# S5 tables of an encoder trunk: products moved from GpSimd to VectorE, sums to accumulating DMAs

## Chip, cores and metric

The kernel runs on 1 core of one Trainium2 chip. The metric is the device time of one execution in microseconds (us). The time before is the median of 3 runs, 1194.32 us (1193.07 to 1194.72). "Contended" below means that VectorE and GpSimd work at the same moment.

## The reference, cut to what matters

One layer, 1024 tokens of width 1024, in float32:

```python
n = rmsnorm(h, norm1_g); proj = n @ w_in
xa, ga, ub, pc = split(proj)          # RG-LRU input and gate, S5 input, Hyena inputs
ya = rglru_mixer(xa, ga, ...)         # conv, 4 gate products, forward and backward linear recurrence
yb = s5_mixer(ub, ...)                # below
yc = hyena_mixer(pc, ...)             # conv, long filter by FFT
h = h + concat(rms(ya), rms(yb), rms(yc)) * g @ w_out
h = h + conv_ffn(rmsnorm(h), ...);    return rmsnorm(h)
```

The S5 mixer has 24 groups of 16 channels, each with one diagonal complex state of 64 values, run forward and backward. The kernel cuts the 1024 tokens into 128 chunks of 8. What a state gets from a chunk, and what a chunk gets from a state, are then small matrices: a power (0 to 8) of the state's complex decay times an entry of B or C. These matrices are the tables of this case.

## The kernel before

**Stages.** `program` (L1459) first normalises x and transposes it. It then walks over 15 column blocks of `w_in` (`names`, L1489: ub0, xa0, ub1, ub2, ga0, xa1, x10, v0, ga1, ...), each in two halves of 512 tokens. One half is 24 matmuls (`columns`, L692: every float32 product is made of three matmuls on a high and a low part, `mm3`, L96). Behind each block its consumer takes the PSUM result: `s5_in` for ub, `rg_conv` for xa, `rg_gate` for ga, `hy_in` for the Hyena blocks. All S5 and RG-LRU work lies between these blocks. Later come the Hyena transforms, the output projection (`wo`) and the ConvFFN, which takes the second half of the time.

**What sets the order.** TensorE's order is the program's own (L1463). The dictionary `before` (L1565) writes it by hand: the entry 2i + half names what is issued ahead of that half of block i. On every other engine the compiler's scheduler picks the order of the queue by its own simulated times, so work that is ready sooner can be issued ahead of work that stands earlier in the program. `tc.issue_after(ins)` puts what a block of code issues on the engine of `ins` behind `ins` in that engine's queue; it is an order in the queue, and no wait for a result. `after` (L1466) opens it for several instructions.

**S5's parts**, for six batches b of 4 groups:

- `prep` (L153), once, on VectorE, makes the powers LPr and LPi and copies them (L279 to L283) into `s5pw` and `s5ow` as (power j, group g), so that the 8 powers of one group lie 24 elements apart.
- `comb` (L302) makes one table of 128 x 512 (4 groups x 16 channels x 8 powers): a product `out = w1 m1` and a product `ox = w2 m2` (L308), and their sum or difference (L310), all on the engine that it is given.
- `lag_prep` (`lp`, L321) makes two tables, Or and Oi, by `comb` on GpSimd, and stores both to DRAM (`s5ot`, L326, on SyncE's DMA queue).
- `lags` (`lg`, L328) multiplies Or and Oi with B on TensorE (`lk`, L339).
- `tables` (`tb`, L364) makes two tables `wn` by `comb`, on VectorE for b below 2 and on GpSimd for the others. It makes the angles `ang` (L380 to L382, VectorE), their sines on ScalarE, and R (L389, a GpSimd product that only spreads rho over 128 columns).
- `transposed` (`wt`) transposes wn on TensorE; `states` (`st`, L432) makes the chunk states: matmuls S, rotations `pr` on VectorE (L451 to L454), scans G (L467, L469), rotations `hr` (L451 to L454); `outputs` (`ou`, L476) multiplies into Y (L485 to L487).

The tables live in a pool of 23 half-size buffers (`half`, L64, L1523), used in turn; a new tile waits until the old one in its buffer has been read.

**The RG-LRU's first input.** `rg_conv` (L740) for block xa0 makes the convolution u (ScalarE L706, VectorE L712 three times), splits it into uh (ScalarE, L87) and ul (VectorE, L88 in `split`), and splits the gate weights wg in the same way. `scan(0, 0)`, at entry 6, multiplies uh and ul with wg (tile `gate`): TensorE issues it right behind the 48 matmuls of block ub1.

**Weights.** Most weight blocks are split by `dsplit` (L90): ScalarE writes lo = -raw, a DMA on GpSimd's queue adds raw onto lo (L93, `accum_op=ALU.add`), and ScalarE writes hi. This accumulating DMA is the kind that the change uses for sums.

Of the kernel before, what the change touches and what calls it, by code (L numbers as in the profile page):

```python
# [10 lines left out]
F32 = mybir.dt.float32  # L11
F32R = mybir.dt.float32r
AF = mybir.ActivationFunctionType
ALU = mybir.AluOpType
# [3 lines left out]
P = 128  # L18
# [9 lines left out]
NG = 24  # L28
# [5 lines left out]
class K:  # L34
# [50 lines left out]
    def split(self, hi, lo, raw, eng=None):  # L85

        self.nc.scalar.activation(hi, raw, AF.Identity)  # L87
        (eng or self.nc.vector).tensor_tensor(lo, raw, hi.bitcast(F32), op=ALU.subtract)  # L88

    def dsplit(self, hi, lo, raw):  # L90

# [14 lines left out]
def bc(ap, *shape):  # L106
    return ap.to_broadcast(list(shape))
# [36 lines left out]
class S5:  # L144
# [8 lines left out]
    def prep(self, tp):  # L153

        k = self.k
        nc = k.nc
        pp = self.pool
        p = self.p1
# [4 lines left out]
        V = nc.vector  # L163
        cnt = [0]

        def t(shape=(P, NG), name=None):
            cnt[0] += 1
            return (pp if name else tp).tile(list(shape), F32, name=name or f"s5t{cnt[0]}")
# [6 lines left out]
        def mul(a, b, out=None):  # L175
            return tt(a, b, ALU.mult, out)
# [91 lines left out]
        for m in (1, 2, 4):  # L268
            S = (P, m, NG)
            cmul(LPr[:, 1:1 + m], LPi[:, 1:1 + m], bc(LPr[:, m:m + 1], *S), bc(LPi[:, m:m + 1], *S),  # L270
                 LPr[:, 1 + m:1 + 2 * m], LPi[:, 1 + m:1 + 2 * m], S)
        m2 = mul(mag, mag)
# [2 lines left out]
        mul(m4, m4, self.rho)  # L275
        self.PW, self.OW = [], []
        for i, LP in enumerate((LPr, LPi)):
            w = t((P, 8, NG), f"s5pw{i}")
            V.tensor_copy(w[:64], LP[:64, 7::-1])  # L279
            V.tensor_copy(w[64:], LP[64:, 0:8])  # L280
            o = t((P, 8, NG), f"s5ow{i}")
            V.tensor_copy(o[:64], LP[:64, 1:9])
            V.tensor_copy(o[64:], LP[64:, 8:0:-1])  # L283
            self.PW.append(w)
            self.OW.append(o)

        self.B2 = []
# [11 lines left out]
        self.Cn = t(S3, "s5cn")  # L299
        V.tensor_scalar(self.Cn, self.ci, -1.0, None, op0=ALU.mult)  # L300

    def comb(self, eng, out, b, w1, m1, w2, m2, op):  # L302

        sh = (P, GB, 16, 8)
        g = slice(GB * b, GB * b + GB)
        x = self.k.half("ox", shape=sh)
        for o, w, m in ((out, w1, m1), (x, w2, m2)):
            eng.tensor_tensor(o, bc(w[:, :, g].rearrange("p j g -> p g j").unsqueeze(2), *sh),  # L308
                              bc(m[:, g].unsqueeze(3), *sh), op=ALU.mult)
        eng.tensor_tensor(out, out, x, op=op)  # L310

    def out_matrix(self, b):

        OT = []
        for n, m1, m2 in (("Or", self.cr, self.ci), ("Oi", self.Cn, self.cr)):
            o = self.k.half(n, shape=(P, GB, 16, 8))
            self.comb(self.k.nc.gpsimd, o, b, self.OW[0], m1, self.OW[1], m2, ALU.subtract)
            OT.append(o)
        return OT

# [43 lines left out]
    def tables(self, b):  # L364

        k = self.k
        nc = k.nc
        S = (P, GB, P)
        V, G = nc.vector, nc.gpsimd
        g = slice(GB * b, GB * b + GB)  # L370
        t = self.tab[b] = {}

        t["W"] = []
        for m1, m2, op in ((self.Gr, self.Gi, ALU.subtract), (self.Gi, self.Gr, ALU.add)):
            w = k.half("wn", shape=(P, GB, 16, 8))
            self.comb(V if b < 2 else G, w, b, self.PW[0], m1, self.PW[1], m2, op)
            t["W"].append(w)

        ang, rnd = k.half("ang", shape=S), k.half("rnd", shape=S)
        V.tensor_tensor(ang, bc(self.f8s[:, g].unsqueeze(2), *S), bc(self.nt.unsqueeze(1), *S), op=ALU.mult)  # L380
        V.tensor_scalar(rnd, ang, MAGIC, -MAGIC, op0=ALU.add, op1=ALU.add)
        V.tensor_tensor(ang, ang, rnd, op=ALU.subtract)  # L382
        Es, Ec, R = t["Es"], t["Ec"], t["R"] = [k.half(n, shape=S) for n in ("Es", "Ec", "R")]
        one = k.col(1.0, "c_one")
        nc.scalar.activation(Es, ang, AF.Sin, scale=2.0 * PI_LO)
        nc.scalar.activation(Ec, ang, AF.Sin, scale=PI_LO)
        nc.scalar.activation(Ec, Ec, AF.Square)
        nc.scalar.activation(Ec, Ec, AF.Identity, scale=-2.0, bias=one)
        G.tensor_tensor(R, bc(self.rho[:, g].unsqueeze(2), *S), bc(one, P, 512).rearrange("p (g n) -> p g n", n=P),  # L389
                        op=ALU.mult)  # L390
        G.memset(R[0:64, :, 0], 0.0)
        G.memset(R[64:128, :, 127], 0.0)

# [213 lines left out]
class Net:  # L607
# [132 lines left out]
    def rg_conv(self, ct, ps):  # L740
        k = self.k
        u = self.conv(ps, [self.c("rcw", 3 * j + ct) for j in range(4)], self.c("rcb", ct), 1, "u")
        uh, ul = k.slot("uh", F32R), k.slot("ul", F32R)
        k.split(uh, ul, u)
        wgs = []
        for d in range(2):
            wg = k.half("wg", F32R, (P, 2, 256))
            raw = k.half("wgr", shape=(P, 256))
            k.nc.sync.dma_start(raw, self.I["gates"][ct][:, 256 * d:256 * d + 256])
            k.split(wg[:, 0], wg[:, 1], raw)  # L750
            wgs.append(wg)
        return u, uh, ul, wgs
# [359 lines left out]
class Ffn:  # L1112
# [36 lines left out]
    def second(self, ns):  # L1149
# [11 lines left out]
        for kt in range(4):  # L1161
            p12, p22 = self.transposes(ns, kt), self.transposes(ns, kt + 4)
            g1, g2 = self.net.c("n2", kt), self.net.c("n2", kt + 4)
            b22 = k.half("b22")
            nc.scalar.activation(b22, p22, AF.Identity, scale=g2)  # L1165
            t1, t3 = k.half("t1"), k.half("t3")
            V.scalar_tensor_tensor(t1, p12, g1, f(self.B11[kt][0]), op0=ALU.mult, op1=ALU.subtract)
            V.scalar_tensor_tensor(t3, p12, g1, b22, op0=ALU.mult, op1=ALU.subtract)
            split(self.B22[kt], b22, V)
            V.tensor_tensor(t1, t1, f(self.B11[kt][1]), op=ALU.subtract)  # L1170
            t2 = k.half("t2")
            V.tensor_tensor(t2, b22, t1, op=ALU.subtract)
            split(self.T2[kt], t2, V)
            split(self.T3[kt], t3, V)
            split(self.T1[kt], t1, G)
            G.tensor_tensor(t2, f(self.B21[kt][0]), t2, op=ALU.subtract)
            G.tensor_tensor(t2, t2, f(self.B21[kt][1]), op=ALU.add)
            split(self.T4[kt], t2, V)
            yield
# [279 lines left out]
def program(ctx, tc, I, O, dbg=None):  # L1459
    k = K(ctx, tc)  # L1460
    nc = k.nc
    net = Net(k, I, O)
    ctx.enter_context(tc.manual_schedule(engines={mybir.EngineType.PE}))  # L1463

    @contextmanager
    def after(*instructions):  # L1466

        with ExitStack() as st:
            for i in instructions:
                st.enter_context(tc.issue_after(i))  # L1470
            yield
# [16 lines left out]
    x = [k.slot(f"x{i}") for i in range(8)]  # L1488
# [66 lines left out]
    def load(src, o):  # L1555
        for i in range(src.shape[0]):
# [3 lines left out]

    lp, lg, il, tb, wt, st, lo = (s5.lag_prep, s5.lags, s5.intra_load, s5.tables, s5.transposed, s5.states,
                                  s5.load_out)
    lu, ou = lambda b: s5.load_u(b, part(ud, b)), lambda b: s5.outputs(b, part(yd, b))

    before = {  # L1565
        2: [(lp, 0), (lp, 1)],
        4: [(lp, 2), (net.hy_layer, 1)],
        6: [(scan, 0, 0)],
        7: [(lg, 0), (tb, 0)],
        8: [(tb, 1), (lg, 1)],  # L1570
        9: [(il, 0), (scan, 0, 1), (lp, 3)],
        10: [(lg, 2)],
        11: [(wt, 0), (lu, 0), (lo, 0)],
# [187 lines left out]
```

## Time and profile before

| what | us |
|---|---|
| median of 3 runs | 1194.32 |
| the profiled execution, its own time | 1192.28 |
| its span, first to last instruction | 1190.5 |
| granted TensorE clock, mean over the span | 0.958 of full speed |

One execution was profiled; all times within it are in us from the first instruction. The trace gives each instruction with its engine, its line, the tiles that it writes and reads (out<-in), its duration and what ended the idle time before it. PE is TensorE, PEld its weight loads, DVE VectorE, ACT ScalarE, POOL GpSimd, SPq and POOLq the DMA queues of SyncE and GpSimd. A line such as L88 or L308 is that of a helper, so the tile tells what it serves. Merged rows (x2, x24) give a common start and total length.

### The profile page before, as it was taken

How to read it: one execution, taken by the hardware profiler on the slowest of the kernel's cores; microseconds unless marked ns; L12 is line 12 of the kernel's file. 1: busy time of each engine (PE TensorE's matmuls, PEld its weight loads, DVE VectorE, ACT ScalarE, POOL GpSimd, SP SyncE). 2: the span in 40 equal slices, each digit the busy share in tenths (PEclk: the TensorE clock that was granted, in tenths of full speed). 3: DMA queues.
4: the chain of work that ended last, by engine and by line, in shares of the span. 5: the costliest groups of instructions: out<-in, count | busy, mean ns of one | idle time of the engine just before them, and what ended most of it. 6: DMA issues, size and time to landing. Idle time of an engine off the chain costs nothing.

```text
span 1190.5 us, 13485 instructions
## 1 busy us (share of the span) xinstructions
PE 1083.7 (91%) x4938; PEld 880.1 (74%) x4938; DVE 1016.7 (85%) x1246; ACT 543.1 (46%) x757; POOL 441.2 (37%) x330
## 2 busy tenths in 40 slices
PE   5849989987998989968999999999999998999896
PEld 4638877766686778756878888888888876888785
DVE  6997689998879984997989898988989899578975
ACT  6429566555241550643434343343434353545453
POOL 6285375342317442375433232323232234011002
PEclk8969999988988999988999999999999999999998
DMA  6233724525736151311322222222212590455003
GB/s 246 62 107 90 219 56 134 131 77 159 257 110 237 36 198 52 158 36 35 106 80 80 89 72 92 79 95 71 89 71 89 190 357 18 135 142 114 1 1 142
DMA packets 58511, 134.27 MB, mean 113 GB/s; under 512 B 10923, under 2 KB 19499, under 8 KB 58444
## 3 DMA queue, kind: packets, MB, share of 16 engines
q1 hardware_dynamic: 53116, 114.00, 27.9%
q0 software_dynamic: 5328, 19.40, 7.0%
q8 instruction: 39, 0.64, 0.2%
q14 instruction: 28, 0.23, 0.1%
HBM read 96.24 MB, written 30.33 MB: 106 GB/s over the span
## 4 chain that ended last, share of the span: by engine, by line
PE 45%; DVE 21%; issue 11%; ACT 3%; POOL 2%; DMA 2%; SPq 0%; POOLq 0%; DVEq 0%; ACTq 0%
PE p L97 31%; PE dn L97 5%; PE wo L97 5%; DVE dr L1299 2%; DVE dw L88 2%; PE x L97 1%; DVE G L469 1%; DMA wor<-in_w_out 1%; DVE T L1159 1%; DVE S L88 1%; DVE hrm L451 1%; DVE hrn L453 1%; DVE cv L712 1%; DVE B L1159 1%; DMA dr<-gd 1%
## 5 line engine op out<-in xcount | busy, mean ns | idle before, releaser
L97 PE MATMUL dn<-dw 128*128 128x512 f32 x924 | 213.8, 393 | 10.0 <-DVE dw L88 9.9
L97 PEld LDWEIGHTS dn<-dw 128*128 128x128 f32 x924 | 173.9, 189 | 49.7 <-DVE dw L88 13.3
L97 PE MATMUL p<-T,S 128*128 128x512 f32 x792 | 188.7, 397 | 3.0 <-DVE T L1159 3.0
L97 PEld LDWEIGHTS p<-T,S 128*128 128x128 f32 x792 | 150.5, 190 | 37.6 <-DVE T L1159 3.4
L87 ACT ACTIVATE dw<-dr 128x512 fp32r<-128x512 f32 x154 | 88.2, 624 | 106.2 <-PE dn L97 92.2
L97 PE MATMUL p<-B,A 128*128 128x512 f32 x528 | 131.0, 403 | 5.0 <-ACT b L1165 3.1
L97 PEld LDWEIGHTS p<-B,A 128*128 128x128 f32 x528 | 101.3, 193 | 30.1 <-ACT b L1165 3.3
L88 DVE TENSOR_TENSOR dw<-dr,dw 128x512 fp32r<-128x512 f32 x154 | 101.1, 706 | 22.5 <-ACT dw L87 22.5
L1203 POOL TENSOR_TENSOR upv<-upv,upg 128x512 f32<-128x512 f32 x22 | 48.1, 2186 | 194.2 <-DVE upv L1202 193.8
L97 PE MATMUL wo<-wo,y 128*128 128x512 f32 x384 | 95.2, 409 | 7.6 <-DVE wo L1037 3.9
L1259 POOL TENSOR_TENSOR cv<-cv 128x1024 f32<-128x1024 f32 x22 | 76.7, 3484 | 60.0 <-DVE cv L712 47.4
L97 PEld LDWEIGHTS wo<-wo,y 128*128 128x128 f32 x384 | 74.6, 196 | 26.6 <-DVE wo L1037 5.0
L87 ACT ACTIVATE S<-upg 128x1024 fp32r<-128x1024 f32 x22 | 23.3, 1060 | 121.2 <-DVE upg L1205 109.5
L712 DVE SCALAR_TENSOR_TENSOR cv<-uv,cols,cv 128x1023 f32<-128x1023 f32 x44 | 75.1, 1707 | 0.8
L97 PE MATMUL p<-B,S 128*128 128x512 f32 x264 | 65.9, 399 | 5.2 <-ACT b L1165 4.1
L97 PE MATMUL p<-T,A 128*128 128x512 f32 x264 | 66.8, 403 | 2.9 <-DVE z L1245 2.9
L97 PEld LDWEIGHTS p<-B,S 128*128 128x128 f32 x264 | 50.4, 192 | 17.6 <-ACT b L1165 4.6
L97 PEld LDWEIGHTS p<-T,A 128*128 128x128 f32 x264 | 50.4, 191 | 15.3 <-DVE z L1245 3.4
L1299 DVE TENSOR_TENSOR dr<-dr 128x1024 f32<-128x1024 f32 (+1 forms) x48 | 53.0, 1130 | 7.1 <-DMA dr<-gd 7.1
L88 DVE TENSOR_TENSOR A<-upg,A 128x1024 fp32r<-128x1024 f32 x20 | 58.5, 2924 | 0.0
L103 POOL TENSOR_TENSOR rs<-ms,c_mhalf 128x1 f32<-128x1 f32 x24 | 14.2, 596 | 116.8 <-DVE ms L629 112.0
L712 DVE SCALAR_TENSOR_TENSOR cv<-ug,cols,cv 128x1023 f32<-128x1023 f32 x44 | 56.3, 1279 | 0.7 <-ACT cv L706 0.7
(387 smaller groups left out, 2185.4 us busy)
## 6 DMA issues: line engine op xcount, KB each, us to landing
upg<-in_w_up SPq DMA_DIRECT2D x22, 512.0 KB, 3.3
upv<-in_w_up SPq DMA_DIRECT2D x22, 512.0 KB, 3.4
gd<-cv SPq DMA_DIRECT2D x22, 512.0 KB, 2.6
dr<-gd SPq DMA_DIRECT2D x20, 512.0 KB, 8.6
dr<-in_w_down SPq DMA_DIRECT2D x20, 512.0 KB, 8.2
x<-in_x SPq DMA_DIRECT2D x8, 512.0 KB, 7.2
dft<-in_dftf POOLq DMA_DIRECT2D x8, 512.0 KB, 8.1
wor<-in_w_out SPq DMA_DIRECT2D x8, 512.0 KB, 7.0
```

Of the source, the lines that this page charges most:

```text
L87: self.nc.scalar.activation(hi, raw, AF.Identity)
L88: (eng or self.nc.vector).tensor_tensor(lo, raw, hi.bitcast(F32), op=ALU.subtract)
L97: mm = lambda *a, **b: self.nc.tensor.matmul(*a, **b, **kw)
L103: self.last_pow = self.nc.gpsimd.tensor_tensor(out, base, expo, op=ALU.pow).ins
L451: V.tensor_tensor(m, a, t["Ec"], op=ALU.mult)
L453: V.tensor_tensor(m2, c, t["Es"], op=ALU.mult)
L469: V.tensor_tensor_scan(o[64:128, 510::-1], r[64:128, 511:0:-1], x[64:128, 511:0:-1], initial=0.0, op0=ALU.mult, op1=ALU.add)
L712: k.nc.vector.scalar_tensor_tensor(o[:, dst], ps[:, src], w, o[:, dst], op0=ALU.mult, op1=ALU.add)
L1159: eng.tensor_tensor(op[1], raw, f(op[0]), op=ALU.subtract)
L1203: G.tensor_tensor(a21, a21, a11, op=ALU.subtract)
L1259: G.tensor_tensor(o[0], o[0], o[1], op=ALU.mult)
L1299: self.k.nc.vector.tensor_tensor(B(o), B(x), B(y), op=f)
```

## The change

- The powers are stored as (group, power), so that a group's 8 powers lie side by side, and the imaginary part of `s5ow` is negated once in `prep`.
- `comb` makes both products on VectorE for every table. Where a difference is wanted (the real `wn`, one table in each of the six batches) VectorE subtracts. The other 18 sums (Or, Oi and the imaginary `wn`) are made by a DMA of GpSimd's queue that adds `ox` onto `out`.
- R is made by ScalarE.
- `lp` of batches 0 to 2, the second Hyena layer and `tb` of batches 0 and 1 are issued behind `ul` of block xa0 on VectorE (`later`). For this `lp` 0 and 1 move from entry 2 to entry 4, and `lp` 2 from entry 4 to entry 5.

```diff
     def split(self, hi, lo, raw, eng=None):
 
         self.nc.scalar.activation(hi, raw, AF.Identity)
-        (eng or self.nc.vector).tensor_tensor(lo, raw, hi.bitcast(F32), op=ALU.subtract)
+        return (eng or self.nc.vector).tensor_tensor(lo, raw, hi.bitcast(F32), op=ALU.subtract).ins
...
-            w = t((P, 8, NG), f"s5pw{i}")
-            V.tensor_copy(w[:64], LP[:64, 7::-1])
...
+            w, o = t((P, NG, 8), f"s5pw{i}"), t((P, NG, 8), f"s5ow{i}")
+            jg = lambda a: a.rearrange("p g j -> p j g")
+            V.tensor_copy(jg(w[:64]), LP[:64, 7::-1])
...
+            if i:
+                V.tensor_scalar(o, o, -1.0, None, op0=ALU.mult)
...
-    def comb(self, eng, out, b, w1, m1, w2, m2, op):
+    def comb(self, out, b, w1, m1, w2, m2, subtract=False):
+
+        V = self.k.nc.vector
         sh = (P, GB, 16, 8)
         g = slice(GB * b, GB * b + GB)
         x = self.k.half("ox", shape=sh)
         for o, w, m in ((out, w1, m1), (x, w2, m2)):
-            eng.tensor_tensor(o, bc(w[:, :, g].rearrange("p j g -> p g j").unsqueeze(2), *sh),
+            V.tensor_tensor(o, bc(w[:, g].unsqueeze(2), *sh),
                               bc(m[:, g].unsqueeze(3), *sh), op=ALU.mult)
-        eng.tensor_tensor(out, out, x, op=op)
+        if subtract:
+            V.tensor_tensor(out, out, x, op=ALU.subtract)
+        else:
+            self.k.nc.gpsimd.dma_start(out, x, accum_op=ALU.add)
...
-            self.comb(self.k.nc.gpsimd, o, b, self.OW[0], m1, self.OW[1], m2, ALU.subtract)
+            self.comb(o, b, self.OW[0], m1, self.OW[1], m2)
...
-        for m1, m2, op in ((self.Gr, self.Gi, ALU.subtract), (self.Gi, self.Gr, ALU.add)):
+        for m1, m2, subtract in ((self.Gr, self.Gi, True), (self.Gi, self.Gr, False)):
             w = k.half("wn", shape=(P, GB, 16, 8))
-            self.comb(V if b < 2 else G, w, b, self.PW[0], m1, self.PW[1], m2, op)
+            self.comb(w, b, self.PW[0], m1, self.PW[1], m2, subtract)
...
-        G.tensor_tensor(R, bc(self.rho[:, g].unsqueeze(2), *S), bc(one, P, 512).rearrange("p (g n) -> p g n", n=P),
-                        op=ALU.mult)
+        nc.scalar.activation(R, bc(self.rho[:, g].unsqueeze(2), *S), AF.Identity)
...
-        k.split(uh, ul, u)
+        self.last_ul = k.split(uh, ul, u)
...
+    def later(f, b):
+
+        with after(net.last_ul):
+            f(b)
+
     before = {
-        2: [(lp, 0), (lp, 1)],
-        4: [(lp, 2), (net.hy_layer, 1)],
+        4: [(later, lp, 0), (later, lp, 1), (later, net.hy_layer, 1)],
+        5: [(later, lp, 2)],
         6: [(scan, 0, 0)],
-        7: [(lg, 0), (tb, 0)],
-        8: [(tb, 1), (lg, 1)],
+        7: [(lg, 0), (later, tb, 0)],
+        8: [(later, tb, 1), (lg, 1)],
```

## Rows read from the trace of the kernel before

**Rows 1.** Stretches: their length, busy PE, PEld, DVE, ACT, POOL; clock, DMA share, GB/s.

```profile
65.20:82.10 16.90, 0.06 (x2) 0.05 (x1) 16.90 (x7) 2.31 (x2) 16.53 (x12) 0.57 0.51 155
...
93.30:150.00 56.70, 56.70 (x352) 47.53 (x352) 38.98 (x50) 40.48 (x48) 29.17 (x28) 1.00 0.62 163
...
230.00:280.00 50.00, 35.57 (x163) 29.47 (x162) 47.74 (x41) 28.43 (x31) 29.95 (x29) 0.89 0.37 94
...
330.00:430.00 100.00, 90.88 (x458) 76.11 (x456) 88.12 (x98) 41.87 (x53) 44.39 (x30) 0.95 0.42 146
```

**Rows 2.** PE in order of time: start, length, instruction, idle before it.

```profile
54.02 11.19 PE L97 MATMUL ub<-n,ub1w 128*128 128x512 f32 x48
...
82.06 0.80 PE L97 MATMUL gate<-ul,wg 128*128 128x512 f32 x1 [16.84 <-DVE ul L88]
...
87.34 5.99 PE L97 MATMUL ub<-n,ub2w 128*128 128x512 f32 x24
...
108.60 0.39 PE L97 MATMUL gate<-ul,wg 128*128 128x512 f32 x1
...
111.36 5.63 PE L97 MATMUL ga<-n,ga0w 128*128 128x512 f32 x24
```

**Rows 3.** DVE in order of time, from the first convolution on.

```profile
54.36 3.92 DVE L712 SCALAR_TENSOR_TENSOR u<-xa,cols,u 128x1023 f32<-128x1023 f32 x3 [1.07 <-ACT u L706]
58.20 2.05 DVE L308 TENSOR_TENSOR wn<-s5pw,s5Gr 128x512 f32<-128x512 f32 x1
...
68.93 10.48 DVE L88 TENSOR_TENSOR wg<-wgr,wg 128x256 fp32r<-128x256 f32 x2
...
79.94 2.06 DVE L88 TENSOR_TENSOR ul<-u,uh 128x1024 fp32r<-128x1024 f32 x1
...
90.30 1.42 DVE L308 TENSOR_TENSOR ox<-s5pw,s5Gr 128x512 f32<-128x512 f32 x1
...
92.23 0.68 DVE L380 TENSOR_TENSOR ang<-s5f8s,s5p 128x512 f32<-128x512 f32 x1
```

**Rows 4.** ACT in order of time: two splits, and a pass of 512 columns.

```profile
57.70 1.06 ACT L92 ACTIVATE ub2w<-ub2r 128x1024 fp32r<-128x1024 f32 x1 [3.37 <-DMA ub2r<-in_w_in]
...
60.23 1.05 ACT L87 ACTIVATE uh<-u 128x1024 fp32r<-128x1024 f32 x1
...
96.03 0.72 ACT L388 ACTIVATE Ec<-Ec,c_one 128x512 f32<-128x512 f32 x1
```

**Rows 5.** Tiles hrm and m, one row each: ns min/median/max, first and last start.

```profile
L454 DVE TENSOR_TENSOR hrm<-hrm,hrn x12: 680/685/1954, 156.4 to 325.6; 128x512 f32<-128x512 f32 x12
...
L777 DVE SCALAR_TENSOR_TENSOR m<-gt,m x6: 1220/1450/2482, 96.1 to 266.5; 128x1024 f32<-128x1024 f32 x6
```

**Rows 6.** POOL in order of time: the issue of an accumulating DMA.

```profile
70.08 0.89 POOL L93 DMA_DIRECT2D ub2w<-ub2r  x1
```

**Rows 7.** DMA issues, KB each, median us to landing.

```profile
s5ot<-Or SPq DMA_DIRECT2D x4, 256.0 KB, 2.3
...
ub2w<-ub2r POOLq DMA_DIRECT2D x1, 512.0 KB, 6.0
```

**Rows 8.** DVE beside POOL's tables of batch 5: first and last of seven instructions.

```profile
262.30 2.42 DVE L773 SCALAR_TENSOR_TENSOR gt<-gt,u 128x1024 f32<-128x1024 f32 x1
...
274.13 1.99 DVE L380 TENSOR_TENSOR ang<-s5f8s,s5p 128x512 f32<-128x512 f32 x1
```

**Rows 9.** PE's waits from 150 to 290 us: total, times, longest.

```profile
PE Y L486 <- DVE hrm L454: 8.6, 2, 6.2
...
PE Y L487 <- DVE hrm L454: 2.3, 2, 1.4
PE x L97 <- DVE q L712: 2.1, 1, 2.1
```

**Rows 10.** A stretch behind the longest of these waits (columns as in rows 1).

```profile
276.00:282.00 6.00, 4.28 (x18) 3.99 (x19) 6.00 (x9) 3.72 (x5) 0.00 (x0) 0.50 0.76 191
```

**Rows 11.** A POOL group, 45 to 290 us: total, mean ns, idle before and releaser.

```profile
L308 POOL TENSOR_TENSOR Or<-s5ow,s5p 128x512 f32<-128x512 f32 x6 | 10.0, 1669 | 6.7 <-PE lk L339 5.7 <-DVE s5ow L283 1.0
```

More of the change, by code (lines that the diff above doesn't have):

```diff
@@ L277, in prep @@
         for i, LP in enumerate((LPr, LPi)):
-            w = t((P, 8, NG), f"s5pw{i}")
-            V.tensor_copy(w[:64], LP[:64, 7::-1])
[L280 to L283, printed above, removed]
+            w, o = t((P, NG, 8), f"s5pw{i}"), t((P, NG, 8), f"s5ow{i}")
+            jg = lambda a: a.rearrange("p g j -> p j g")
+            V.tensor_copy(jg(w[:64]), LP[:64, 7::-1])
+            V.tensor_copy(jg(w[64:]), LP[64:, 0:8])
+            V.tensor_copy(jg(o[:64]), LP[:64, 1:9])
+            V.tensor_copy(jg(o[64:]), LP[64:, 8:0:-1])
             self.PW.append(w)
+            if i:
+                V.tensor_scalar(o, o, -1.0, None, op0=ALU.mult)
             self.OW.append(o)
```

## The prediction

> **What bounds the kernel now.** I read the stretches of busy time first, then TensorE's order of time where it idles, then VectorE's and ScalarE's order there, then TensorE's waits. The stretches show three regimes [rows 1]. From 65.2 to 82.1 us TensorE does nothing, while VectorE and GpSimd are both full. From 93.3 to 150 TensorE is busy for all 56.7 us and VectorE for 39.0. From 230 to 280 VectorE is the full engine (47.7 of 50) and TensorE has 14.4 us of holes. From 330 to 430 both run near 90%, so time gained earlier has no idle stretch there in which to vanish.
>
> The hole at 65.2 is one wait: TensorE ends block ub1 at 54.02 + 11.19 = 65.21 and its gate products start at 82.06, released by ul [rows 2]. ul's operands were ready long before: u at 54.36 + 3.92 = 58.28 [rows 3], uh at 60.23 + 1.05 = 61.28 [rows 4]. But VectorE took table products from 58.20 on, and then two splits of wg, 256 columns each, that took 10.48 us [rows 3]; a pass of 512 columns takes 0.68 at its best and 1.95 at its worst, one of 1024 columns 1.22 and 2.48 [rows 5]. The slow cases lie beside GpSimd's products, which fill 16.53 us of this hole [rows 1]. So the reader should see two costs: a queue order (ul behind tables that are not urgent), and two engines that slow each other.
>
> **Part 1: ul first.** With `lp` 0 to 2, `tb` 0 and 1 and the second Hyena layer behind ul, VectorE finds wg, then ul. ul starts when uh is there, 61.3, and takes 1.2 (the uncontended 1024 columns of [rows 5]; its own 2.06 in [rows 3] was contended), so it ends at 62.5, 2.7 us before TensorE needs it. The 16.84 us go. The gate products ran from 82.06 to 87.34, 5.28 us, in a stretch with a mean granted clock of 0.57 behind it; the same products at the next scan took 108.60 to 111.36, 2.76 [rows 1, 2]. I take the latter: another 2.5. The next half block falls from 5.99 to 5.63: 0.4. Part 1 is worth 16.84 + 2.52 + 0.36 = **19.7 us**.
>
> What is late next? The weights ub2w are wanted at 65.2 + 2.8 = 68.0. Before, their accumulating DMA was issued at 70.08 behind GpSimd's products [rows 6]; ScalarE's lo is ready at 58.76 [rows 4], and GpSimd's queue is now empty, so with 6.0 to landing [rows 7] they are there at 64.8. Then the lags of batch 0 want Or and Oi at 68.0 + 5.7 = 73.7. Four products behind ul end at 62.5 + 4 x 0.68 = 65.2, two issues of 0.89 [rows 6] bring the second add to 66.1 at the earliest. An add of 256 KB onto a tile in SBUF is not in the trace; the nearest rows are 2.3 (a plain 256 KB store) and 6.0 (512 KB, accumulating) [rows 7]. I take 4, since 256 KB is half of the accumulating one. It lands at 70, and at the upper end at 72.1: covered, by 1.6 at worst. Behind this comes the stretch in which TensorE alone is full and VectorE has 17.7 us free [rows 1], so the 19.7 us are carried through it; the 8 products of `lp` 3 and 4 (5.4 us) fit into that slack. The moved Hyena layer has no reader until the signals behind the last column block.
>
> **Part 2: products on VectorE.** All 48 products are now VectorE's, 12 batches of 4, and 6 subtractions. Price of one: not in the trace. Its powers come in runs of 8 adjacent words, repeated 16 times, its other operand is repeated over each run. The lower end is 0.68, a pass of 512 whose two operands are both repeated; the upper is 1.42, the present product with its powers 24 words apart [rows 3]. I take 0.68, because runs of neighbours are nearer to that row. The Trainium skill (Vector Engine (DVE) Microarchitecture Reference, "Measured stream behaviour on trn2") gives 1.054 ns per column for runs of two or more adjacent words and 2.50 for a step of 24 words; by that the sum would be the same, and no run here shows it yet.
>
> In the VectorE-bound region the tables of batches 2 to 5 leave GpSimd. The one batch that I work out: seven VectorE instructions from 262.30 to 274.13 + 1.99 = 276.12 take 13.8 us [rows 8]; uncontended, five of 512 and two of 1024 columns take 5 x 0.68 + 2 x 1.22 = 5.8 [rows 5]. So 8.0 are lost to contention. Each batch adds 4 x 0.68 + 0.68 = 3.4 of new work. At the least a batch loses the two hrm instructions' 2 x 1.27 = 2.5 [rows 5]. Four batches therefore change VectorE's load by between 4 x (3.4 - 2.5) = +3.6 and 4 x (3.4 - 8.0) = -18.4, and `lp` 5 adds 2.7. I take 8.0 for two batches and the middle, 5.2, for two: 26.4 - 13.6 - 2.7 = 10.1. TensorE's side allows it: its waits on hrm and q there sum to 13.0 [rows 9], and behind the longest, 6 us run at half clock with 4.28 busy [rows 10], another 2.1. Part 2 is worth **10.1 us**, between -6.3 and 15.1.
>
> **Parts costed at nothing.** R on ScalarE: 6 passes of 0.72 [rows 4], 4.3 us, beside an engine busy 28 of 50 [rows 1]; uncovered, 4.3. The changed copies and one negation in `prep` lie where VectorE still waits 1.07 for ScalarE's u [rows 3]. The 18 adds cost GpSimd 18 x 0.89 = 16 us of issue, in place of its products; what is queued behind an add that waits for its product is the next weight add and the memsets of G, which wait for VectorE anyway. On SyncE's queue the 12 stores of Or and Oi now wait for a landing (4 us) instead of a GpSimd sum, and weight loads stand behind them; they start some 20 us earlier, which is the cover. Without it each store could hold a load by 4.
>
> **Sum.** 1192.28 (the profiled execution) - 19.7 - 10.1 = 1162.5. The median of the runs stands 2.0 above that execution, so the forecast is **1164.5 us**.
>
> **Rivals.**
> - *Only the first hole closes.* Behind 150 us the products eat what contention gives back, as the low bound of part 2 allows. For it: VectorE is full there. Against: 8.0 measured in one batch. 1194.3 - 19.7 = 1174.6.
> - *The products keep their price of 1.42.* 20 of them behind 150 us cost 0.74 more each, 14.8, so part 2 turns to +4.7: 1179.3. For it: no row has this pattern. Against: `ang`.
> - *The adds land late.* Each of the six lags waits 6.0 - 2.3 = 3.7 longer than a store would make it: 22.2 at most, up to 1186.7. For it: batch 0 has only 1.6 to spare. Against: the issue on GpSimd took 0.89 beside a full VectorE. The Trainium skill (SBUF — State Buffer, "SBUF: two separate sides") speaks against this change here: while VectorE runs a two-port operation, GpSimd cannot write the descriptors of its DMAs, 620 ns becoming 3100 in its example, by which (an estimate) six lags would lose 15 and the time would be 1179; the issue of 0.89 does not show it.
> - *Slower: VectorE stops in its queue for a buffer.* The pool has 23 buffers, and a table waits for the old tile's readers. GpSimd waited 5.7 us for one, on the lag products [rows 11], at no cost. The same wait on VectorE holds everything behind it. Ten batches come to it; six such waits (34) use up the gain of 29.8, all ten give 1221.5. Against: GpSimd met one such wait in all of its tables.
> - *The order does not hold ul first.* If tables stay ahead of it, 12 products (8.2) and wg put ul at 68.5, 3.3 behind TensorE: 1168.
>
> **Chances.** Forecast 0.54 (its own range 1156 to 1171), only the first hole 0.20, dear products 0.07, late adds 0.09, buffers 0.05, order 0.05. The range runs from 1151 (part 2 at its upper bound, and some of the holes between 280 and 430 as well) to 1180 (which takes in the dear products and half of the late adds); 0.86 of the chance lies near it, less its tails. Faster by over 0.2% (2.4 us, about what a measurement of this kernel can tell from no change): 0.91; within it 0.03; slower 0.06, nearly all of it the buffers.
>
> **What would show it.** In the changed profile: ul ends near 62.5 and no wait stands before the first gate product; a product of 128x512 takes 0.68; hrm's longest falls from 1.95 to 0.69; the waits of Y on hrm fall below 5 in all; the lags wait for no add. A second hole before 150, products near 1.4, or VectorE idle on PE lk or on a DMA in front of L308 would make the prediction wrong.

## The result, and the profile after

| kernel | median us (runs) | ratio to before, 95% interval |
|---|---|---|
| before, in the same job | 1194.52 (4) | 1 |
| changed | 1168.74 (1163.62 to 1171.44, 4) | 0.9776 [0.9754, 0.9797] |
| changed, measured again in a later job | 1170.83 (1165.39 to 1174.37, 6) | 0.9805 [0.9775, 0.9834] |

The change saves 26 us; 1164.5 was forecast, between 1151 and 1180. The profiled execution of the changed kernel is the slowest of its four: its own time is 1171.44, its span 1169.7, its granted clock 0.963.

The same four stretches as in [rows 1], with the same columns (length, busy PE, PEld, DVE, ACT, POOL; clock, DMA share, GB/s):

```profile
65.20:82.10 16.90, 16.43 (x94) 13.22 (x93) 14.74 (x28) 10.55 (x13) 7.05 (x8) 1.00 0.97 218
93.30:150.00 56.70, 46.17 (x260) 37.44 (x259) 42.43 (x54) 38.37 (x45) 7.07 (x17) 0.96 0.69 177
230.00:280.00 50.00, 43.47 (x220) 36.06 (x218) 45.93 (x52) 31.20 (x38) 7.81 (x28) 0.97 0.49 141
330.00:430.00 100.00, 89.25 (x421) 72.83 (x420) 93.28 (x98) 43.09 (x51) 55.47 (x32) 0.91 0.49 170
```

The first stretch has turned over: TensorE went from 0.06 to 16.43 of 16.90, GpSimd from 16.53 to 7.05. In the third, TensorE went from 35.57 to 43.47. But the second, in which TensorE was full, now has 10.5 us of holes. That is the part to explain.

VectorE's order of time ahead of the first gate products (start, length, instruction, idle before it):

```profile
61.53 0.43 DVE L88 TENSOR_TENSOR wg<-wgr,wg 128x256 fp32r<-128x256 f32 x1 [1.50 <-ACT wg L87]
62.48 1.23 DVE L88 TENSOR_TENSOR ul<-u,uh 128x1024 fp32r<-128x1024 f32 x1 [0.53 <-ACT uh L87]
63.62 0.68 DVE L312 TENSOR_TENSOR Or<-s5ow,s5p 128x512 f32<-128x512 f32 x1
```

TensorE's order there:

```profile
59.79 6.97 PE L97 MATMUL ub<-n,ub1w 128*128 128x512 f32 x30
66.60 0.39 PE L97 MATMUL gate<-ul,wg 128*128 128x512 f32 x1
...
69.30 0.50 PE L97 MATMUL gate<-ul,wg 128*128 128x512 f32 x1 [0.47 <-DVE ha L880]
...
70.10 4.06 PE L97 MATMUL ub<-n,ub2w 128*128 128x512 f32 x17
```

`ul` stands ahead of every table, takes 1.23 and ends at 63.7. The wait of 16.84 [rows 2] is gone. Of the gate products only the fourth group waits, 0.47, and for `ha`, an instruction of the moved Hyena layer. `gate` reads nothing of `ha`; both take a PSUM bank from `bank`, and that is what they can share.

More than half of the old hole was a single instruction. Of the two splits of wg before it (10.48 us in [rows 3]) one took 1.48 and the other 9.08, from 70.3 to 79.4, for 256 columns; six GpSimd instructions ran one behind the other from 70.69 to 79.12:

```profile
L88 DVE TENSOR_TENSOR wg<-wgr,wg x2: 1479/5281/9083, 68.9 to 70.3; 128x256 fp32r<-128x256 f32 x2
```

In the changed kernel these splits take 0.41 and 0.43. So a contended pass is not only doubled: it can last as long as a row of GpSimd's instructions.

The changed kernel's instructions that write or read `ox`, with min/median/max in ns and first and last start, and the waits that the view names:

```profile
L312 DVE TENSOR_TENSOR ox<-s5ow,s5p x12: 680/682/692, 64.2 to 156.4; 128x512 f32<-128x512 f32 x12
L317 POOL DMA_DIRECT2D Or<-ox x6: 862/872/1584, 65.2 to 156.4; - x6
L317 POOL DMA_DIRECT2D wn<-ox x6: 872/872/1565, 74.6 to 251.6; - x6
...
  DVE prm L457: 2.6, 1
...
DMA to landing us min/median/max: 3.3/5.7/12.9
```

and the rotation of [rows 5]:

```profile
L460 DVE TENSOR_TENSOR hrm<-hrm,hrn x12: 678/682/691, 144.1 to 303.8; 128x512 f32<-128x512 f32 x12
```

A product takes 0.68 in every case, as taken, and hrm's longest fell from 1.95 to 0.69. Over the span VectorE has more instructions and less busy time, and GpSimd loses 103 us of its 441.2:

```profile
PE 1080.7 (92%) x4938; PEld 876.9 (75%) x4938; DVE 988.4 (85%) x1289; ACT 545.3 (47%) x763; POOL 338.2 (29%) x282
```

Before, VectorE had 1016.7 busy in 1246 instructions.

**Where the time came from, and where some went back.** TensorE's order is the same in both kernels, so I subtract the start of the same instruction. The first gate product moves from 82.06 to 66.60 (-15.5), ub2 from 87.34 to 70.10 (-17.2). The lags of batch 0 stand at -17.6, and this holds up to 117 us of the old trace. Then the lags of batch 2 are at -14.7, the second half of v0 (163.90 to 153.96) at -9.9 and the lags behind it at -9.3. So 8.3 us are given back. Later the offset grows again, behind 165 us: -16.5 at ga2, -26.4 in the middle of ga2 (282.71 to 256.28; there the old wait of Y stood), and about -22 to -24 from there on; the spans differ by 20.8. These offsets carry one that is not the change's: in the repeat (e12 below), the same kernel, the first gate product starts at 63.50, 3.1 sooner. From 39.2 to 45.0 us the granted clock is 0.50 (1.2 GHz) in this execution and 1.00 (2.4 GHz) in the repeat, with a mean of 0.71 in the kernel before, behind the same waits of 0.5 to 1.1 us, and the 24 matmuls of ub0 that follow take 8.06 against 5.78.

TensorE's waits between 60 and 310 us (waiter, releaser, total, times, longest) show by what:

```profile
PE wtps L414 <- ACT gt L774: 4.8, 1, 4.8
...
PE Y L493 <- DVE hrm L460: 4.1, 1, 4.1
PE Y L492 <- DMA intrar<-s5lag: 3.5, 1, 3.5
PE k L350 <- ACT gt L774: 2.7, 1, 2.7
```

The wait for k (at 102.67) is the first loss; the two of Y (144.87 and 149.67) are the second: they sum to 7.6, where the kernel before waited 2.4 and 1.4 at the same place. The third row shown names a DMA, but the rotation that this Y reads ends at 144.14 + 0.68 = 144.82, 0.05 before Y starts, so I read it as a wait for VectorE too. What holds ScalarE and VectorE up is seen in their own order. ScalarE, ahead of k:

```profile
97.47 0.69 ACT L774 ACTIVATE gt<-gate,hcols 128x512 f32<-128x512 f32 x1
...
98.70 1.28 ACT L886 ACT_TABLE_LOAD   x1
99.99 0.63 ACT L886 ACTIVATE hid<-ha 128x512 f32<-128x512 f32 x1
100.64 1.28 ACT L774 ACT_TABLE_LOAD   x1
101.94 1.84 ACT L774 ACTIVATE gt<-gate,hcols 128x512 f32<-128x512 f32 x3
```

VectorE, ahead of Y:

```profile
131.49 0.69 DVE L457 TENSOR_TENSOR prm<-S,Ec 128x512 f32<-128x512 f32 x1 [2.56 <-DMA Oi<-ox]
...
144.14 0.68 DVE L460 TENSOR_TENSOR hrm<-hrm,hrn 128x512 f32<-128x512 f32 x1
...
147.13 0.68 DVE L312 TENSOR_TENSOR wn<-s5pw,s5Gr 128x512 f32<-128x512 f32 x1
147.73 0.68 DVE L312 TENSOR_TENSOR ox<-s5pw,s5Gi 128x512 f32<-128x512 f32 x1
148.33 0.68 DVE L312 TENSOR_TENSOR wn<-s5pw,s5Gi 128x512 f32<-128x512 f32 x1
148.94 0.68 DVE L460 TENSOR_TENSOR hrm<-hrm,hrn 128x512 f32<-128x512 f32 x1
```

The sine of the second Hyena layer splits the gate tanhs and stands between two table loads (rows ACT_TABLE_LOAD, 1.28 us each, where ScalarE goes over to another function). Before, the same sine stood right behind the sines of batch 1's angles and needed no load of its own, as ScalarE's order in the old kernel shows:

```profile
98.53 1.28 ACT L385 ACT_TABLE_LOAD   x1
99.83 0.63 ACT L385 ACTIVATE Es<-ang 128x512 f32<-128x512 f32 x1
...
101.02 0.63 ACT L880 ACTIVATE hid<-ha 128x512 f32<-128x512 f32 x1
```

On VectorE a rotation waits 2.56 for the buffer that an adding DMA still reads, and three products of batch 2's tables stand ahead of the last rotation that Y needs.

### The profile page after: what moved, and what is told of

Read it like the earlier page. It is cut to its first block, busy times and chain, and to the rows that moved or that the text cites. A ratio compares the mean times of both kernels' runs of the same rounds, so it can differ in the third digit from the quotient of the medians.

```text
span 1169.7 us, 13490 instructions
## 1 busy us (share of the span) xinstructions
PE 1080.7 (92%) x4938; PEld 876.9 (75%) x4938; DVE 988.4 (85%) x1289; ACT 545.3 (47%) x763; POOL 338.2 (29%) x282
## 4 chain that ended last, share of the span: by engine, by line
PE 48%; DVE 25%; issue 12%; DMA 6%; ACT 6%; POOL 4%; POOLq 0%; DVEq 0%; SPq 0%; ACTq 0%
PE p L97 30%; PE dn L97 6%; PE wo L97 4%; DVE dr L1305 2%; DVE dw L88 2%; DVE G L475 1%; DMA wn<-ox 1%; DVE G L473 1%; DMA dr<-gd 1%; PE xa L97 1%; PE ub L97 1%; DVE T L1165 1%; POOL rs L103 1%; DVE S L88 1%; DVE n L682 1%
## 5 line engine op out<-in xcount | busy, mean ns | idle before, releaser
L97 PE MATMUL dn<-dw 128*128 128x512 f32 x924 | 216.4, 396 | 9.3 <-DVE dw L88 9.2
L97 PEld LDWEIGHTS p<-T,A 128*128 128x128 f32 x264 | 50.6, 192 | 15.4 <-DVE z L1251 3.4
```

Source lines behind the costliest of these rows:

```text
L97: mm = lambda *a, **b: self.nc.tensor.matmul(*a, **b, **kw)
```

## The experiments

### Are the two parts worth what the sum says?

`e1_order_only` is the old kernel with the new order alone (tables still made as before); `e2_no_order` is the changed kernel with the old order.

```diff
 e1: before.py
-        2: [(lp, 0), (lp, 1)],
-        4: [(lp, 2), (net.hy_layer, 1)],
+        4: [(later, lp, 0), (later, lp, 1), (later, net.hy_layer, 1)],
+        5: [(later, lp, 2)],
...
-        7: [(lg, 0), (tb, 0)],
-        8: [(tb, 1), (lg, 1)],
+        7: [(lg, 0), (later, tb, 0)],
+        8: [(later, tb, 1), (lg, 1)],
 e2: the same lines of the changed kernel, the other way round
```

> The kernel before with the order alone: lp 0 to 2, the second Hyena layer and tb 0 and 1 behind ul on VectorE, tables otherwise as before (GpSimd products for lp, powers 24 apart, R on GpSimd). Theory (two separate costs, queue order and contention): ul moves up, but lp's products on GpSimd still run beside wg and ul, so of the 16.8 us hole some 12 close and the region from 150 to 290 us keeps its holes: 1180 us (1176 to 1184). Rival 1 (the order is the whole gain): 1169, no slower than the changed kernel. Rival 2 (contention alone made the hole, the order is idle): 1194.

> The changed kernel without the order: tables on VectorE with powers side by side, sums by adding DMAs, R on ScalarE, but the hand-written order of the kernel before and nothing held behind ul. Theory: VectorE issues up to 12 products (8 us), some of them ahead of ul, at 0.68 each, so a hole of about 3 to 8 us stays before the first gate product: 1174 us (1171 to 1178). Rival 1 (the order is the whole gain): 1190 or more. Rival 2 (contention alone): 1169, as the changed kernel.

Measured: e1 1207.14, ratio 1.0082 [1.0050, 1.0114]; e2 1176.92, ratio 0.9829 [0.9800, 0.9858]. e2 came as expected; e1 missed its theory and both rivals: the order alone is a loss. The waits of TensorE in e1 (60 to 310 us) tell why:

```profile
PE ub L97 <- DMA ub2w<-ub2r: 8.6, 1, 8.6
PE ga L97 <- ACT ga0w L94: 8.1, 1, 8.1
...
PE ga L97 <- DMA ga0w<-ga0r: 5.4, 1, 5.4
```

`ul` was early there too (the gates started at 66.67, 15.4 sooner than before), and TensorE then stopped at ub2, whose weights are completed by an accumulating DMA on GpSimd's queue. It stood behind the table products that GpSimd still had to make:

```profile
71.48 2.43 POOL L308 TENSOR_TENSOR ox<-s5ow,s5p 128x512 f32<-128x512 f32 x1
73.86 0.89 POOL L93 DMA_DIRECT2D ub2w<-ub2r  x1
```

In the old kernel the same DMA was issued at 70.08 [rows 6] and hidden, because TensorE itself stood until 82.06. So the hole did not close, it moved from a wait for VectorE to a wait for GpSimd's queue. To test that, e9 takes ub2 (alone) off that queue: its lo is made by a VectorE subtraction, as ub0's and xa0's are.

```diff
-        (k.split if nm in ("ub0", "xa0") else k.dsplit)(hi, lo, raw)
+        (k.split if nm in ("ub0", "xa0", "ub2") else k.dsplit)(hi, lo, raw)
```

> The order alone (as in the run with the order alone), with one edit more: the weights ub2 are split by ScalarE and VectorE (as ub0 and xa0 are), so that no adding DMA for them stands in GpSimd's queue behind lp's products. Theory: in the run with the order alone the hole only moved, from the gates to the weights ub2 (8.6 us, their add issued behind 12 products on GpSimd) and then to the weights ga0 (8.1 and 5.4 us, ScalarE held in its queue by contended VectorE work). Without the add the 8.6 us wait is gone, and the raw weights ga0 are loaded some 10 us earlier; the ga0 wait stays in part: 1199 us (1192 to 1202). Rival (the holes come from the later scan work, whatever the weights): 1207, and a hole of 8 us still before block ub2.

Measured: 1199.33, ratio 1.0038 [1.0021, 1.0055]. The time came as expected, but not in the way that was expected: the wait for ub2w is gone, those for ga0w, which were to stay in part, are gone too, and a wait of the gate products for `lks` on VectorE, 12.9 us in two pieces, takes their place. With GpSimd full of products beside VectorE, one freed wait uncovers the next. The two parts of the change aren't additive: order alone +0.8%, products alone -1.7%, both -2.2% (-1.95% when measured again). What the order adds to the products is thus 3 to 6 us, and the interval of e2 touches that of the second measurement, so it is not certain.

### What carries the second part?

`e4_powers_apart` leaves everything of the change but stores the powers 24 words apart, as before.

```diff
-            w, o = t((P, NG, 8), f"s5pw{i}"), t((P, NG, 8), f"s5ow{i}")
-            jg = lambda a: a.rearrange("p g j -> p j g")
+            w, o = t((P, 8, NG), f"s5pw{i}"), t((P, 8, NG), f"s5ow{i}")
+            jg = lambda a: a
...
-            V.tensor_tensor(o, bc(w[:, g].unsqueeze(2), *sh),
+            V.tensor_tensor(o, bc(w[:, :, g].rearrange("p j g -> p g j").unsqueeze(2), *sh),
```

> The changed kernel with the powers stored as before, 24 elements apart. Theory: a product takes 1.42 us again, 0.74 more; of the 48 products the 20 behind 150 us lie where VectorE is full (14.8 us) and some of the first 20 delay the gates of the first scan: 1186 (1180 to 1192). Rival (VectorE has room for them, the layout is worth little): 1170 to 1174.

Measured: 1190.88, ratio 0.9955 [0.9937, 0.9972], inside the expected range. One product now takes 1.42 (columns as above), and this alone gives back four fifths of the gain:

```profile
L312 DVE TENSOR_TENSOR ox<-s5ow,s5p x12: 1416/1419/1430, 65.0 to 172.9; 128x512 f32<-128x512 f32 x12
```

and of TensorE's waits (60 to 310 us) two are:

```profile
PE Y L493 <- DVE hrm L460: 6.2, 1, 6.2
PE gate L97 <- DVE ha L880: 6.2, 1, 6.2
```

The dearer products push `ha` back and with it the gate products (0.5 in the changed kernel), and the wait for hrm grows from 4.1 to 6.2. The forecast's rival of dear products is hereby a measured case, and its price of 14.8 was too low: (0.9955 - 0.9776) x 1194.5 = 21.4. The gate's wait for `ha` of 6.2 was not in that price.

`e3_sums_vector` and `e5_sums_gpsimd` make the 18 sums by an instruction instead of a DMA, on VectorE and on GpSimd.

```diff
-        if subtract:
-            V.tensor_tensor(out, out, x, op=ALU.subtract)
-        else:
-            self.k.nc.gpsimd.dma_start(out, x, accum_op=ALU.add)
 e3:
+        V.tensor_tensor(out, out, x, op=ALU.subtract if subtract else ALU.add)
 e5:
+        (V if subtract else self.k.nc.gpsimd).tensor_tensor(out, out, x, op=ALU.subtract if subtract else ALU.add)
```

> The changed kernel with all 24 sums by VectorE, none by an adding DMA: 18 additions of 0.60 us, 10.8 us more on VectorE, of which some 5 lie where it is full. Theory: the adding DMAs cost little beside the 2.6 us wait of prm for a buffer that one of them held, so it comes out 2 to 6 us slower: 1173 (1170 to 1176). Rival (the DMAs' late landings, up to 12.9 us, and the full DMA queues from 65 to 93 us are what eats the gain between 100 and 165 us): 4 to 8 us faster, 1162.

> The changed kernel with the 18 sums as GpSimd instructions of 512 columns in place of adding DMAs. Theory (contention is what GpSimd's work costs VectorE): 18 instructions of 1.3 to 2.3 us come back beside a full VectorE, each can double one VectorE instruction, 0.7 to 1.2 us each, about half on the path: 6 to 12 us slower than the changed kernel, 1178. Rival (only the products mattered; sums are cheap wherever they are): within 3 us of it, as the sums on VectorE were.

Measured: e3 1170.33, ratio 0.9779 [0.9748, 0.9810], the same as the changed kernel, where the theory had 2 to 6 us more and the rival 4 to 8 less; e5 1171.50, ratio 0.9813 [0.9772, 0.9854], between theory and rival, and its interval holds the changed kernel's ratio. So the adding DMAs are worth nothing that these runs can tell from sums on VectorE or GpSimd: what counts is the products. That the two engines slow each other does show in e5's trace, where GpSimd's sums lie beside VectorE's products. From 63 to 78 us six products take 1.60 to 1.78 instead of 0.68, each begun 0.4 to 0.6 us behind the start of a sum; one pair:

```profile
63.72 1.78 DVE L312 TENSOR_TENSOR ox<-s5ow,s5p 128x512 f32<-128x512 f32 x1
...
63.29 1.66 POOL L314 TENSOR_TENSOR Or<-Or,ox 128x512 f32<-128x512 f32 x1 [3.56 <-DVE ox L312]
```

In e3 the rotation's wait for a DMA is gone, but 18 more passes of 0.68 lie on VectorE, and Y waits 5.0 for hrm.

### What gives the 8 us back behind 102 us?

Two suspects on VectorE first. e6 issues the tables of batch 2 behind the last rotation of the first states; e7 gives `ox` two buffers of its own, with 21 instead of 23 left for the rest.

```diff
 e6:
-                V.tensor_tensor(m, m, m2, op=op)
+                self.last_rot = V.tensor_tensor(m, m, m2, op=op).ins
...
+    def behind(f, b):
+        with after(s5.last_rot):
+            f(b)
-        13: [(lu, 1), (st, 0), (tb, 2)],
+        13: [(lu, 1), (st, 0), (behind, tb, 2)],
 e7:
-        x = self.k.half("ox", shape=sh)
+        x = self.k.get("x", "ox", shape=sh)
-    k.open(s5st, "halves", t=23)
+    k.open(s5st, "halves", t=21, x=2)
```

> The changed kernel with VectorE's tables of batch 2 issued behind the last rotation hrm of the first chunk states. Theory: three table products (1.8 us) and nothing else of the tables stood between hrm and its end at 149.6, so the second wait of Y falls from 4.1 to about 2.3 and the end comes up to 2 us earlier: 1166 to 1168. Rival (the time is given back at the next wait on VectorE): 1169, no difference.

> The changed kernel with two buffers of their own for ox and 21 instead of 23 for the rest. Theory: prm waited 2.6 us for a buffer that an adding DMA still read; with ox outside the pool that wait goes, but ox's two buffers now turn at the DMAs' pace (landings of 3.3 to 12.9 us), so the products of lp 1 and 2 wait up to 6 us for them behind ul, ahead of work of the first scan: between 2 us faster and 5 us slower, 1170 (1167 to 1174). Rival (buffers never matter): 1169 with the prm wait gone and no new wait.

Measured: e6 1165.92, ratio 0.9759 [0.9724, 0.9793]; e7 1182.15, ratio 0.9893 [0.9858, 0.9928]. In e6 the wait of the second Y fell from 4.1 to 2.3, exactly the three products; the first Y waits 4.3 instead of 3.5. e6's interval overlaps the changed kernel's, so this run alone doesn't decide. e7 was a miss: 13 us slower than the changed kernel, where at most 5 were expected. prm no longer waits for an adding DMA, as expected, but VectorE now meets, ten times and for 5.1 in all, the kind of wait that the forecast's slower rival had named (VectorE's waits, 60 to 310 us, columns as above):

```profile
DVE kzr L902 <- DMA dec<-in_decay: 5.8, 1, 5.8
...
DVE ox L312 <- DMA Or<-ox: 2.6, 4, 1.5
...
DVE ox L312 <- DMA Oi<-ox: 1.8, 4, 1.1
...
DVE ox L312 <- DMA wn<-ox: 0.7, 2, 0.5
```

TensorE waits 6.6 before Y for a signal of the Hyena filter (kzr) and 6.5 for hrm. The run made two edits at once, `ox`'s pair of buffers and 21 in place of 23 for the rest; how the 13 us split between them isn't shown. As tried, a dedicated pair is no remedy.

The third suspect is the moved Hyena layer. `e13_hyena_later` issues it at entry 10, ahead of the lags of batch 2; `e11_both_moves` adds e6's edit; `e12_changed_again` is the changed kernel itself; `e14_table2_again` is e6's edit once more. e11 and e12 ran on one chip, e13 and e14 on one.

```diff
-        4: [(later, lp, 0), (later, lp, 1), (later, net.hy_layer, 1)],
+        4: [(later, lp, 0), (later, lp, 1)],
...
-        10: [(lg, 2)],
+        10: [(net.hy_layer, 1), (lg, 2)],
```

> The changed kernel with two moves: the tables of batch 2 behind the last rotation of the first states (as in the run before), and the second Hyena layer issued at entry 10 instead of entry 4, behind ScalarE's second group of gate tanhs. My theory says that the wait of 2.7 us before the lag product k at 102.7 us stands there because ScalarE's sine of that layer takes 0.63 and two table loads of 1.28 (3.2 in all) out of the middle of the tanhs; with the sine later the wait falls below 0.5, and the start of k comes 2.5 earlier. How much of this is left behind 150 us depends on Y of batch 0, which waits for VectorE and not for TensorE: 1163 to 1166, where the move of the tables alone had 1165.9 and the changed kernel 1168.7. The rival, that another instruction of ScalarE takes the place of the sine (the weights xa1w stand in the same queue), keeps the wait and the time at 1166 to 1169.

> The changed kernel itself once more, to be set beside the run with both moves on the same chip. Theory: its median lies at 1168 to 1169 and its ratio at 0.977 to 0.979, 2.4 us or more above the kernel with both moves; if the moves are worth nothing, the two ratios lie within 0.001 of each other.

> The changed kernel with the second Hyena layer at entry 10 alone; the tables of batch 2 stay where the change put them. Theory: the wait before k at 102.7 goes as in the run with both moves, but three products stand ahead of the last rotation again, so the wait before the second product Y of batch 0 is 1.8 longer than there; the two moves add up, and since both gave a ratio of 0.9707 against 0.9805 of the changed kernel (11.3 us), and the tables' move 2.8 by its own run, this one is worth 7 to 9: a ratio of 0.973 to 0.975. Rival: without the tables' move the time is lost again at Y, which waits for VectorE and not for TensorE, and the ratio is 0.978 or more.

> The changed kernel with the tables of batch 2 behind the last rotation, once more, beside the run with the Hyena layer's move alone on one chip. Theory: ratio 0.977 to 0.979, that is 1 to 3 us below the changed kernel, as 1.8 of wait is all that it removes. Rival: the first run's 0.9759 was the moves' full size, and the Hyena layer's move is worth as much or less.

| kernel | median us | ratio, 95% interval |
|---|---|---|
| changed, again (e12) | 1170.83 | 0.9805 [0.9775, 0.9834] |
| batch 2's tables behind (e14) | 1166.08 | 0.9739 [0.9716, 0.9762] |
| Hyena layer later (e13) | 1161.48 | 0.9716 [0.9693, 0.9739] |
| both (e11) | 1159.57 | 0.9707 [0.9680, 0.9733] |

No interval of the three touches that of e12; those of e13 and e11 don't touch the changed kernel's first one either (e14's does, as e6's did). The Hyena layer's place is worth 7 to 11 us by these ratios (e13 against the two of the changed kernel), where e11's expectation had only 2.5 at k. e11, e13 and e14 all came out better than their theories, and e12 about 2 us slower than its own. By their times the two moves don't add up: e13 and e11 can't be told apart. In the stretch that lost the time they nearly do. From the start of ub2 to the second half of v0 the kernel before takes 76.6 us, the changed kernel 83.9 and 83.8 in its two profiles, with batch 2's tables behind 82.3 (e6) and 81.2 (e14), with the Hyena layer later 79.8, with both 78.6. So of 7.3 us lost there, the layer's place accounts for about 4 and the tables' for 1.5 to 2.7; 2 are left. What is left of TensorE's waits in e13, 60 to 310 us:

```profile
PE wtps L414 <- ACT gt L774: 4.7, 1, 4.7
PE Y L493 <- DVE hrm L460: 4.3, 1, 4.3
...
PE Y L492 <- DVE hrm L460: 1.9, 1, 1.9
```

The waits for k, for `ha` and for u are gone, and the first Y waits 1.9 instead of 3.5. ScalarE's tanhs run through:

```profile
92.01 0.69 ACT L774 ACTIVATE gt<-gate,hcols 128x512 f32<-128x512 f32 x1
92.59 0.62 ACT L394 ACTIVATE Ec<-Ec 128x512 f32<-128x512 f32 x1
93.11 1.84 ACT L774 ACTIVATE gt<-gate,hcols 128x512 f32<-128x512 f32 x3
```

The sine itself still needs a load of its own in e13 (at 107.85), but there the next tanh comes 20 us later.

Against the profile of e12, ub2 starts 1.6 sooner in e13, k 2.8, v0's second half 5.6 and dn 7.1. What stands behind k I read in VectorE's order: the layer's seven instructions lay between the first tables and the first scan's work, and are out of that chain now. The loads and these seven instructions were only moved together, so how the gain splits between them stays open. The runs compare the change's place of the layer with a third one, later; its old place, under the new order, was not run.

## Why the prediction was right, and where it was not

- **The time** was inside the range, 4.2 us above the forecast by the first median and 6.3 by the second. Its nearness is in part luck: by 165 us the trace stands at -9.3 where the whole 19.7 of part 1 were to be carried, and what lies behind adds 12 to 15 where 10.1 were forecast.
- **Its own signs.** No wait stands before the first gate product, a product takes 0.68, hrm's longest fell to 0.69 and no lag waited for an add, as it said; ul ended at 63.7 (62.5 was given). But the waits of Y on hrm were to fall below 5 in all and are 7.6 (4.1 by the labels alone), and a second hole before 150 us, which it named as a sign against itself, did open: 10.5 us of TensorE's holes from 93.3 to 150.
- **Part 1, ul first.** The mechanism held in every step that was named: `ul` started at 62.48 (61.3 was taken), no long wait stands before the gates, and they take 3.5 where they took 5.28, at a granted clock of 1.00 in this stretch. Of 19.7, 17.6 stood in the trace in front of the lags of batch 0: 1.4 is missing because ub1 ends at 66.6 in this execution and not at 65.2 (the lower clock ahead of it, above), and 0.7 because the gates take 3.5 and not 2.76, 0.47 of it the wait for `ha`. The step that failed is "the 19.7 us are carried through it". That stretch, from 93.3 to 150, was judged by TensorE's full row and VectorE's 17.7 us free; once TensorE came 17.6 earlier, ScalarE and VectorE were what was late in it, and 8.3 us went back.
- **The Hyena layer at nothing.** "The moved Hyena layer has no reader until the signals" put the move at nothing; set behind `ul` at entry 4 the layer costs 7 to 11 us against entry 10, by the ratio of e13 against the two of the changed kernel. That its result has no early reader is right, but `gate` waits for its `ha` (0.5 here, 6.2 in e4; by a PSUM bank, as I read it), its sine splits the tanhs with two table loads of 1.28, and its instructions stand in VectorE's queue ahead of the first scan.
- **Part 2, products on VectorE.** The price of 0.68 was right. (The upper bound adds up to 15.7, 4 x 8.0 - 13.6 - 2.7, and not to 15.1; nothing hangs on it.) Its worth was not 10.1: alone (e2) it makes 1.71% of 1194.5, 20.4 us, since with the products off GpSimd the first hole shrinks too, from 16.84 to 4.9 in e2, where each of the splits of wg takes 0.42; that lies in part 1's term. The last rival had this mechanism: `ul` behind 12 products, 3.3 late. The Trainium skill (Vector Engine (DVE) Microarchitecture Reference, "Measured stream behaviour on trn2") was borne out in direction: adjacent runs cost nothing extra, a step of 24 words does (0.68 against 1.42). Its 2.50 is for both sources or the destination at that step; here one source steps.
- **The sum.** Adding the parts was the weak place of the method. Alone they are +9.8 (e1: 0.82%) and -20.4, together -26.8; the sum of 19.7 and 10.1 came near because each term had the other part's gain in it without saying so. Part 1 needs GpSimd's queue free of table products, which only part 2 brings. The prediction said "GpSimd's queue is now empty" in passing; e1 shows what happens without it. Taking ub2's add off that queue (e9) gives back 5 of e1's 9.8 us and still leaves the kernel slower than before, so the queue is not the only condition. With the Hyena layer at entry 10, the order adds 13.5 us to the products (e13 against e2, whose intervals lie apart).
- **The adds.** Issue 0.87 as taken, landing 4.6 to 6.0 by the three kinds' medians instead of 4; no lag waited for one; ScalarE did once, for 1.76 by the label, which the repeat (e12) doesn't show. The rule against the change (the Trainium skill, SBUF — State Buffer, "SBUF: two separate sides") isn't seen in the issues: beside a VectorE that is full they keep their 0.87, and the longest (1.58 and 1.95) stand behind other issues. The rule is for VectorE operations in a two-port mode; for operations with two SBUF inputs, as these products are, the same section names only GpSimd operations that read SBUF, so the prediction took it too far. Whether the late landings owe anything to it, no run here shows.
- **R on ScalarE**, also put at nothing, took 0.61 a pass instead of 0.72; it was not run apart.
- **The slower rival, buffers.** VectorE met one such wait, 2.56 us, and not ten. In e7, with two buffers for `ox` alone, it met ten, and they were short: 5.1 in all.

## What to carry to other kernels

Ask of each part of a change which condition it takes from another part, and forecast the parts alone as well: an engine that is let go early stops at whatever was hidden behind its old wait. A piece of work with no early reader is still not free to move: it has a bank, a place in three queues, and on ScalarE a function table, so put it where nothing urgent stands behind it, or beside work of the same table, as the old kernel had it. And before work is moved onto a busy engine, see to its operands' layout: here the order of the powers in memory, 24 words apart or adjacent, decided four fifths of the gain. Of the versions run, the change with the second Hyena layer at entry 10, with or without batch 2's tables behind the rotations, is faster than both kernels.

## What I had not expected of the hardware

An adding DMA of 256 KB from SBUF onto SBUF landed after 3.3 us at best, 5.7 in the middle and 12.9 at worst. The slow one is the first `wn` add, issued at 74.59, in the stretch with a DMA share of 0.97; whether the share is the cause was not tried. The changed kernel's executions spread over 8 and 9 us in its two jobs, before's over 4 and 7 in the same. Of the 3.3 us between the spans of its two profiled executions, 3.1 stand ahead of the first gate product, where one was granted a clock of 0.50 from 39.2 to 45.0 us and the other 1.00. Why is not shown, and the rest of the spread isn't explained.
